# Attention heads interleaved with projections: which engine prepares weights, norms and pair parts, and in which slot each step stands

## The chip, the cores and the metric

The kernel runs on one core of a Trainium2 chip. The metric is the device time of one execution in microseconds (us). Five engines work side by side, each through its own instructions in a fixed order: TensorE (PE, with its weight loads PEld), VectorE (DVE), ScalarE (ACT), GpSimd (POOL) and SyncE (SP), which here only issues transfers between HBM and the on-chip memory, and within the latter. They wait for each other through semaphores.

## The reference

Two layers on 512 frames of 1024 channels in float32. Layer 0 mixes tokens by pooling, layer 1 by attention with 16 heads of 64 channels; both are followed by a gated MLP of width 2816. The change lies in the attention of layer 1, of which this is what must be computed:

```python
qkv = h @ w_qkv                                   # h: RMS-normed input, (512, 1024)
q, k, v = jnp.split(qkv, 3, axis=-1)
q = head_rmsnorm(q.reshape(B, S, N_HEADS, HEAD_DIM), q_norm)
k = head_rmsnorm(k.reshape(B, S, N_HEADS, HEAD_DIM), k_norm)
...
s = jnp.einsum('bqhd,bkhd->bhqk', qc, kb).astype(jnp.float32) * scale + bias[None]
s = jnp.where(valid[None, None, None, :], s, -1e30)
p = jax.nn.softmax(s, axis=-1).astype(vb.dtype)
return jnp.einsum('bhqk,bkhd->bqhd', p, vb)
...
return o @ w_o
```

A frame attends to its own chunk of 64 frames and the eight chunks before it; `bias` is a clipped relative-position table.

## The kernel before

Every float32 product is made of three fp32r products: an operand is split into a high part (`_h`, a copy rounded to fp32r) and a low part (`_l`, the rest), and `mm3` issues high times high, high times low and low times high. So each weight tile of 128x1024 that a transfer brings (`hw_r`, one per `ask(k)`) needs two further instructions, `parts(k)`: one makes `hw_h`, one subtracts and makes `hw_l`. Tiles k = 0 to 11 are those of the projections of q and k, four each for the head groups c = 1, 2, 3 (group 0 is done before); tiles 12 to 19 are those of the output product `wo`. Before, `hw_h` is made by ScalarE for k below 12 and by GpSimd for 12 to 18, and `hw_l` by GpSimd up to k = 18.

The heads run in a loop over 64 slots: slot i is head i // 4 and query tile t = i % 4 of 128 frames, with (t+1)*128 keys. A slot has two halves, and `place` counts halves. One tile's steps are spread over several slots: PE makes the scores `sc` (two matmuls, L1049 and L1050), VectorE adds the bias tile `B` and finds the maximum (L1054), ScalarE takes the exponential (L1057), VectorE the reciprocal, ScalarE scales (L1061), PE transposes into `tp` (L1065) three slots after the scores, ScalarE and VectorE copy the high and low parts out (L1069, L1071). After a head's four slots PE multiplies with the values (`oo`, L1083); a ScalarE copy and a VectorE add put two heads, a pair p, into one tile `o2` (L1090, L1094), and `split_pair` makes its high part on ScalarE (L1298) and its low part on VectorE (L1302), both in tiles named `two`. `biases(h)` issues the two transfers of a head's bias tile; there are two such tiles, for even and odd heads.

Between these steps `fill` lets PE issue matmuls of the other work, the fillers: the projections of groups 1, 2 and 3 (96 matmuls each, which end at the slots in `FE`), then `outputs()`, 144 matmuls of the output product over pairs 0 to 5. A projection's results are copied out (`copy`), squared and summed per head (`square`, `reduce`), then normed in three steps: `norm`, `seed` (ScalarE) and `better`, whose last act is to scale the four tiles `z` on GpSimd (L1199). Pairs 2c and 2c+1 come from group c.

`stages(p, i)` prepares pair p for its scores (i = 0 is q, 1 is k), in the slots that `CM` names within the eight slots of the pair before: PE transposes `z` into `zt` (L1014), ScalarE scales (L1019, `zf`) and rounds (L1021, `zh`); GpSimd copies half of `zh` (L1023, `z`) and makes the low parts (L1029 `zl` for q, L1027 `kl`, twice, for k); then two transfers from SP move halves between partitions (L1033). The second of them, `zh<-zh`, overwrites what the `kl` steps read, so it waits for both of them; the first scores of the pair, at slot 8p, wait for it.

Apart from these fixed steps, work goes through the lists `waiting`: `later(engine, fn, n)` puts it n places ahead, and `extra(engine)` lets the first entry of that engine's list be issued, in either half of a slot (a second one when the list is long). The whole loop stands in a manual schedule, so that the order of each engine's instructions is what the program writes.

```python
fillers = [(project_heads(1), 96, -3, FE[0]), (project_heads(2), 96, FE[0], FE[1]), (project_heads(3), 96, FE[1], FE[2]), (outputs(), 144, FE[2], nb + FO)]
```

## Time and profile before

| | us |
|---|---|
| median of 3 runs (lowest, highest) | 982.43 (981.92, 983.35) |
| the profiled execution: its own time | 982.51 |
| its span, first to last instruction | 980.7 |
| the stretch of the attention heads in it | 436 to 634 |
| first and last scores (slots 0 and 63) | 452.3, 606.8 |

The profiled execution's own time is 1.8 us over its span and 0.08 us over the median. Times within the span are counted from its first instruction. In rows of the timeline the columns are start, duration, engine, line, operation, output and inputs, shape, and in brackets how long the engine had been idle and what ended that. In rows by stretch, each engine has its busy time and the number of its instructions, and PEclk is the granted clock of TensorE as a share of full speed. Rows of groups have a count, the busy time in all, the mean in ns, and the idle time ahead of them.

### The profile page before, as it was taken

Reading aid. Unit: us, or ns where it says so; the run is one execution under the profiler, and the core shown is the slowest. Engines: PE = TensorE matmul, PEld = TensorE weight load, DVE = VectorE, ACT = ScalarE, POOL = GpSimd, SP = SyncE. Lnnn points to the kernel's source line nnn. Section 1 sums busy time; section 2 is a strip of 40 time slices with the busy share of each in tenths; the row PEclk is TensorE's granted clock in tenths of the full one; section 3 lists DMA queues with packets and bytes.
Section 4 is the critical chain, followed back from the end, with each engine's and each line's share of the span. In section 5 each row is a group of like instructions: output and inputs, shape, how many; then the busy total and the mean of one; then the engine's idle time right before and its main releaser. Section 6 shows DMA issues by size and latency. Waiting matters only on the chain.

```text
span 980.7 us, 13735 instructions
## 1 busy us (share of the span) xinstructions
PE 964.4 (98%) x4982; PEld 817.4 (83%) x4982; DVE 793.9 (81%) x1437; ACT 580.1 (59%) x1005; POOL 137.4 (14%) x116
## 2 busy tenths in 40 slices
PE   9999999999999999999999899999999999999998
PEld 8788988888888888888877787888988888888886
DVE  8999999999899754442665677899989999989953
ACT  7665564654565453355988798646555565556531
POOL 2300000000000022235747553100000000000000
PEclk9999999999999999999999999999999999999999
DMA  9222332332333233233334333323332332332323
GB/s 339 82 86 79 105 113 77 115 118 92 103 110 100 73 98 130 87 108 107 100 86 124 84 75 117 100 70 115 93 113 75 100 132 88 122 95 83 114 83 105
DMA packets 37427, 102.82 MB, mean 105 GB/s; under 512 B 4432, under 2 KB 7904, under 8 KB 37360
## 3 DMA queue, kind: packets, MB, share of 16 engines
q1 hardware_dynamic: 37296, 101.90, 32.7%
q8 instruction: 39, 0.64, 0.3%
q14 instruction: 28, 0.23, 0.1%
q0 software_dynamic: 32, 0.04, 0.0%
q10 hardware_dynamic: 32, 0.00, 0.0%
HBM read 95.60 MB, written 2.14 MB: 100 GB/s over the span
## 4 chain that ended last, share of the span: by engine, by line
PE 89%; DVE 6%; ACT 3%; issue 1%; DMA 1%; POOL 0%; DVEq 0%; SPq 0%; ACTq 0%; POOLq 0%
PE st_m L610 11%; PE out L124 8%; PE out L125 8%; PE out L123 8%; PE st_m L612 6%; PE st_t L610 6%; PE gv L124 3%; PE gv L125 3%; PE gv L123 3%; PE st_t L612 3%; PE st_b L610 3%; PE qk L125 3%; PE qk L123 3%; PE qk L124 3%; PE oo L1083 2%; PE v L124 1%
## 5 line engine op out<-in xcount | busy, mean ns | idle before, releaser
L124 PE MATMUL out<-one,ow_h 128*128 128x512 f32 x224 | 88.0, 393 | 0.0
L123 PE MATMUL out<-one,ow_h 128*128 128x512 f32 x224 | 87.8, 392 | 0.0
L125 PE MATMUL out<-one,ow_l 128*128 128x512 f32 x224 | 87.8, 392 | 0.0
L409 ACT ACTIVATE ow_h<-wo_r 128x640 fp32r<-128x640 f32 (+1 forms) x64 | 50.4, 788 | 56.3 <-PE out L124 46.9
L833 DVE TENSOR_TENSOR X<-out,X 128x512 f32<-128x512 f32 (+1 forms) x65 | 44.1, 679 | 48.9 <-PE out L125 48.8
L1054 DVE CUSTOM_DVE_ANT_0 sb<-sc,B 128x128 f32<-128x128 f32 (+1 forms) x64 | 31.2, 487 | 59.8 <-PE sc L1050 57.1
L610 PE MATMUL st_m<-two,g_h 128*128 128x512 f32 x240 | 75.0, 394 | 0.0
L610 PE MATMUL st_m<-h,g_h 128*128 128x512 f32 x240 | 74.0, 389 | 0.0
L410 DVE TENSOR_TENSOR ow_l<-wo_r,ow_h 128x640 fp32r<-128x640 f32 (+1 forms) x64 | 56.5, 883 | 2.6 <-ACT ow_h L409 2.6
L424 DVE SCALAR_TENSOR_TENSOR c<-a,col,c 128x511 f32<-128x511 f32 (+1 forms) x76 | 56.2, 742 | 0.0
L148 POOL TENSOR_TENSOR n_acc<-n_acc,n_sq 128x512 f32<-128x512 f32 x7 | 9.6, 1368 | 328.1 <-ACT n_sq L146 328.1
L610 PEld LDWEIGHTS st_m<-h,g_h 128*128 128x128 f32 x240 | 45.1, 188 | 10.3
L612 PEld LDWEIGHTS st_m<-two,g_l 128*128 128x128 f32 x240 | 45.0, 188 | 9.5
L610 PEld LDWEIGHTS st_m<-two,g_h 128*128 128x128 f32 x240 | 44.1, 188 | 10.0 <-ACT w L619 0.9
L619 ACT ACTIVATE w<-st_m 128x512 f32<-128x512 f32 x30 | 17.9, 598 | 57.0 <-PE st_m L612 57.0
L103 POOL TENSOR_TENSOR hw_l<-hw_r,hw_h 128x1024 fp32r<-128x1024 f32 x19 | 45.6, 2402 | 27.7 <-ACT hw_h L102 15.3
L612 PE MATMUL st_m<-h,g_l 128*128 128x256 f32 x240 | 48.3, 283 | 0.0
L125 PEld LDWEIGHTS out<-one,ow_l 128*128 128x128 f32 x224 | 42.3, 189 | 6.3
L612 PE MATMUL st_m<-two,g_l 128*128 128x256 f32 x240 | 47.6, 280 | 0.0
L124 PEld LDWEIGHTS out<-one,ow_h 128*128 128x128 f32 x224 | 42.3, 189 | 6.2 <-DVE one L435 0.3
L123 PEld LDWEIGHTS out<-one,ow_h 128*128 128x128 f32 x224 | 42.3, 189 | 6.1
L421 ACT ACTIVATE c<-a,col 128x512 f32<-128x512 f32 x38 | 30.7, 813 | 25.2 <-DVE a L768 23.6
(397 smaller groups left out, 3028.4 us busy)
## 6 DMA issues: line engine op xcount, KB each, us to landing
gv_r<-gv SPq DMA_DIRECT2D x86, 512.0 KB, 3.9
wo_r<-wout SPq DMA_DIRECT2D x32, 384.0 KB, 3.1
wo_r<-wout SPq DMA_DIRECT2D x32, 320.0 KB, 2.9
hw_r<-wqk SPq DMA_DIRECT2D x12, 512.0 KB, 3.8
wv_r<-wv SPq DMA_DIRECT2D x8, 512.0 KB, 3.3
hw_r<-wo SPq DMA_DIRECT2D x8, 512.0 KB, 4.8
xt<-xt SPq DMA_DIRECT2D x4, 512.0 KB, 5.2
X<-xT SPq DMA_DIRECT2D x8, 256.0 KB, 7.4
```

The lines of the kernel that those rows point to most:

```text
L103: return (eng or nc.vector).tensor_sub(lo, raw, hi.bitcast(F32))
L123: yield nc.tensor.matmul(o, sh, mh, start=first, stop=False, **how)
L124: yield nc.tensor.matmul(o, sh, ml, start=False, stop=False, **how)
L125: yield nc.tensor.matmul(o, sl, mh, start=False, stop=last, **how)
L409: nc.scalar.activation(hi[:, :n], raw[:, :n], AF.Copy)
L410: return hi, lo, lambda: nc.vector.tensor_sub(lo[:, :n], raw[:, :n], hi[:, :n].bitcast(F32))
L421: nc.scalar.activation(c, a, AF.Identity, scale=cw[2], bias=cw[3])
L424: nc.vector.scalar_tensor_tensor(c[:, j:], a[:, :S - j], cw[2 - j], c[:, j:], op0=OP.mult, op1=OP.add)
L610: nc.tensor.matmul(o, hi[:, c], B[i, name], start=first and i == 0, stop=False, **how)
L612: nc.tensor.matmul(o[:, 0], lo[:, c], B[i, name][:, 0], start=False, stop=i == 3, **how)
L833: nc.vector.tensor_add(X[d][:, fs], o[:, fs], X[d][:, fs])
L1054: nc.vector.tensor_tensor_reduce(out=s_, in0=sc[:, :n], in1=BT[h % 2][:, :n][:, ::-1], scale=1.0, scalar=3e38, op0=OP.add, op1=OP.min, acc ...
```

## The change

- Projections' weight tiles (k = 0 to 11, tiles 0 to 3 of them ahead of it): `hw_l` moves from GpSimd to VectorE. Output tiles 12 to 18: `hw_h` moves from GpSimd to ScalarE, `hw_l` stays on GpSimd. Past the start, both steps now go through the lists, the low part after the high part, and no longer stand at the matmul that asked for them.
- A list "G" for GpSimd. The norm's steps `norm` and `better` move from VectorE to it (7 instructions on 128x32, one more than before), and so does the pairs' low part (128x512); `norm` follows the last of the four sums, whichever that is. The GpSimd steps of `stages` are issued through it one place after ScalarE's, the transfers as many places after that so that their place stays.
- `FE` is half a slot lower: the projections end sooner by so much, and the outputs begin sooner.
- `CM`: pairs 1, 3, 5, 7 are staged one slot sooner (slots 0 and 1 of eight), pairs 2, 4, 6 one slot later (slots 2 and 3).
- Bias tiles are asked for four slots ahead of their head's first scores, where it was two.
- `outputs()` begins with three output tiles `wo0`, `wo1`, `wo2` over pairs 0 to 2, one tile after the other, then takes pair 3 for all three; before, it was two tiles in turn. The parts of weight tile 14 are asked for seven matmuls later than they would be by the rule for the others.

```diff
@@ -45,9 +45,9 @@
 LAG, LAGM = 3, 2
-FE = (3.5, 19.5, 35.5)
+FE = (3, 19, 35)
 FO = LAG + 6
-CM = (1, 2)
+CM = ((0, 1), (2, 3))
...
@@ -1107,7 +1107,8 @@
         biases(0)
-        w, raws = {}, {}
+        w, raws, ready = {}, {}, set()
+        place = 0
...
@@ -1120,7 +1121,22 @@
             w[k] = [wp.tile([P, 1024], F32R, name=f"hw{k}_{c}", tag=f"w{c}", bufs=2) for c in "hl"]
-            split(raws[k], *w[k], None if k == 19 else nc.gpsimd, nc.gpsimd if 12 <= k < 19 else None)
+            hi, lo = w[k]
+            ready.add(k)
+
+            def make_hi():
+                nc.scalar.activation(hi, raws[k], AF.Copy)
+
+            def make_lo():
+                (nc.gpsimd if 12 <= k < 19 else nc.vector).tensor_sub(lo, raws[k], hi.bitcast(F32))
+                ready.add(k)
+
+            if place == 0 or k == 19:
+                make_hi()
+                make_lo()
+            else:
+                ready.discard(k)
+                later("A", lambda: (make_hi(), later("G" if k >= 12 else "D", make_lo)))
...
@@ -1129,8 +1145,7 @@
         nb = len(tiles_)
-        place = 0
-        waiting = {"A": [], "D": [], "S": []}
+        waiting = {"A": [], "D": [], "G": [], "S": []}
...
@@ -1140,7 +1155,7 @@
             q = waiting[engine]
-            while q and q[0][0] <= place and (n == 0 or all_ or n < 2 and (place < 16 or len(q) > (1 if engine == "D" else 3))):
+            while q and q[0][0] <= place and (n == 0 or all_ or n < 2 and (place < 16 or len(q) > (1 if engine in "DG" else 3))):
...
@@ -1152,7 +1167,7 @@
             ov = {}
-            sums = {}
+            sums, summed = {}, []
...
@@ -1176,25 +1191,27 @@
                 nc.vector.tensor_reduce(three("s")[:, t, :], sq.rearrange("p (h d) -> p h d", d=HD), axis=mybir.AxisListType.X, op=OP.add)
-                if t == TT - 1:
-                    later("D", norm)
+                summed.append(t)
+                if len(summed) == TT:
+                    later("G", norm)
...
             def norm():
-                nc.vector.tensor_mul(three("a"), three("s"), r2[:, :, None].to_broadcast([P, TT, 8]))
-                nc.vector.tensor_scalar(sums["a"], sums["a"], EPS, None, op0=OP.add)
+                nc.gpsimd.tensor_mul(three("a"), three("s"), r2[:, :, None].to_broadcast([P, TT, 8]))
+                nc.gpsimd.tensor_scalar(sums["a"], sums["a"], EPS, None, op0=OP.add)
...
                 nc.scalar.activation(sums["y"], sums["t"], AF.Exp, scale=-0.5)
-                later("D", better)
+                later("G", better)
...
                 a, y, t_ = (sums[v] for v in "ayt")
-                nc.vector.scalar_tensor_tensor(t_, y, -0.5, y, op0=OP.mult, op1=OP.mult)
-                nc.vector.tensor_mul(t_, t_, a)
-                nc.vector.scalar_tensor_tensor(y, t_, 1.5, y, op0=OP.add, op1=OP.mult)
-                nc.vector.tensor_mul(three("y"), three("y"), rcol[:, :, None].to_broadcast([P, TT, 8]))
+                nc.gpsimd.tensor_mul(t_, y, y)
+                nc.gpsimd.tensor_mul(t_, t_, a)
+                nc.gpsimd.tensor_scalar(t_, t_, -0.5, 1.5, op0=OP.mult, op1=OP.add)
+                nc.gpsimd.tensor_mul(y, t_, y)
+                nc.gpsimd.tensor_mul(three("y"), three("y"), rcol[:, :, None].to_broadcast([P, TT, 8]))
...
@@ -1211,6 +1228,7 @@
                         n += 1
+                        assert k in ready
...
@@ -1222,45 +1240,31 @@
-            o = {}
+            o, left = {}, {d: len(ps_) for d in range(KD)}
+            last = ps_[-1]
+            order = [(d, p) for d in range(late) for p in ps_[:-1]] + [(d, last) for d in range(late)]
+            order += [(d, p) for d in range(late, KD) for p in ps_]
             count = 0
-
-            def product(d, p):
-                nonlocal count
-                assert p in kept
+            for d, p in order:
+                assert p in kept and k + d // nd in ready
...
                 s = slice((d % nd * len(ps_) + p - ps_[0]) * P, (d % nd * len(ps_) + p - ps_[0] + 1) * P)
-                for mm in mm3(o[d], hi[:, s], lo[:, s], XS[p], XS[KD + p], p == ps_[0], p == ps_[-1]):
+                for mm in mm3(o[d], hi[:, s], lo[:, s], XS[p], XS[KD + p], p == ps_[0], p == last):
+                    if count % 24 == 0:
+                        chunk(k + count // 24)
+                    if count % 24 == (15 if late and count // 24 == 1 else 8):
+                        parts(k + count // 24 + 1)
                     count += 1
-                    if count % 24 == 1:
-                        chunk(k + count // 24)
-                    if count % 24 == 8:
-                        parts(k + count // 24 + 1)
                     yield mm
-
-            def add(d):
-                later("D", lambda: nc.vector.tensor_add(X[d], o[d], X[d]))
-
-            for d in range(0, KD, late):
-                for p in ps_[:-1] if late > 1 and d == 0 else ps_:
-                    for e in range(d, d + late) if late > 1 and d == 0 else (d,):
-                        yield from product(e, p)
-                if late > 1 and d == 0:
-                    for e in range(late):
-                        yield from product(e, ps_[-1])
-                        add(e)
-                else:
-                    add(d)
-                    for e in range(d + 1, d + late):
-                        for p in ps_:
-                            yield from product(e, p)
-                        add(e)
+                left[d] -= 1
+                if not left[d]:
+                    later("D", lambda d=d: nc.vector.tensor_add(X[d], o[d], X[d]))
...
         def outputs():
-            yield from output_heads(range(4), 12, 2, 2)
-            yield from output_heads((4, 5), 16, 4, 1)
+            yield from output_heads(range(4), 12, 2, 3)
+            yield from output_heads((4, 5), 16, 4, 0)
...
@@ -1296,10 +1300,10 @@
                 nc.scalar.activation(XS[p], O2[p], AF.Copy)
-                later("D", lo)
+                later("G", lo)
...
             def lo():
-                nc.vector.tensor_sub(XS[KD + p], O2[p], XS[p].bitcast(F32))
+                nc.gpsimd.tensor_sub(XS[KD + p], O2[p], XS[p].bitcast(F32))
...
@@ -1325,8 +1329,11 @@
                 next(g)
+                later("G", low)
+
+            def low():
                 next(g)
-                later("S", lambda: run(g), 5 if i else 4)
+                later("S", lambda: run(g), 4 if i else 3)
...
@@ -1336,19 +1343,22 @@
                 step(i, "scores")
-                if i % 4 == 2 and i // 4 + 1 < H:
+                if i % 4 == 0 and i // 4 + 1 < H:
...
                 extra("S")
+                extra("G")
...
                 fill(i + 0.45)
-                if i % 8 in CM and i // 8 + 1 < NPAIR:
-                    stages(i // 8 + 1, CM.index(i % 8))
+                steps_at = CM[i // 8 % 2]
+                if i % 8 in steps_at and i // 8 + 1 < NPAIR:
+                    stages(i // 8 + 1, steps_at.index(i % 8))
...
                 extra("S")
+                extra("G")
...
@@ -1361,11 +1371,12 @@
                 split_pairs()
-            while waiting["A"] or waiting["D"] or cur < len(fillers):
+            while waiting["A"] or waiting["D"] or waiting["G"] or cur < len(fillers):
...
                 extra("D", True)
+                extra("G", True)
...
```

On GpSimd, from the staging of pair 3 on (`z_0`, `zl` are q's, `z_1`, `kl` are k's) to the scaling of the four tiles `z` of group 2. Before:

```order
L1023 CAST z_0_4785<-zh_0_4784 64x512
L1029 TENSOR_TENSOR zl_0_4786<-zf_0_4828,zh_0_4784 128x512
L103 TENSOR_TENSOR hw_l<-hw_r,hw_h 128x1024
L1023 CAST z_1_4826<-zh_1_4825 64x512
L1027 TENSOR_TENSOR kl_3631<-zf_1_4855,zh_1_4825 64x512
L1027 TENSOR_TENSOR kl_3632<-zf_1_4855,zh_1_4825 64x512
L1199 TENSOR_TENSOR z_0_4771<-z_0_4771,qk_y 128x512
```

Now:

```order
L1023 CAST z_0_4756<-zh_0_4755 64x512
L1029 TENSOR_TENSOR zl_0_4757<-zf_0_4800,zh_0_4755 128x512
L1023 CAST z_1_4798<-zh_1_4797 64x512
L1027 TENSOR_TENSOR kl_3631<-zf_1_4834,zh_1_4797 64x512
L1027 TENSOR_TENSOR kl_3632<-zf_1_4834,zh_1_4797 64x512
L1199 TENSOR_TENSOR qk_a<-qk_s,r_3641 128x32
L1200 TENSOR_SCALAR qk_a<-qk_a 128x32
L1210 TENSOR_TENSOR qk_t<-qk_y 128x32
L1211 TENSOR_TENSOR qk_t<-qk_t,qk_a 128x32
L1212 TENSOR_SCALAR qk_t<-qk_t 128x32
L1213 TENSOR_TENSOR qk_y<-qk_t,qk_y 128x32
L1214 TENSOR_TENSOR qk_y<-qk_y,n_y 128x32
```

The weight part between q's and k's steps is gone from GpSimd, and seven small norm steps stand ahead of the scaling.

On ScalarE, around the high part of pair 4 (`two2`), in slots 45 to 47 (`sb11_0` is head 11's tile 0, `pt0h` a high part of the transposes). Before:

```order
L1090 ACTIVATE ob9_5661<-oo9_5652 64x512
L1061 ACTIVATE sb10_3_5617<-sb10_3_5617,mx10_3_5618 128x512
L1069 ACTIVATE pt0h_3625<-tp10_2_5677 128x3x128
L1057 ACTIVATE sb11_1_5668,mx11_1_5669<-sb11_1_5668,mx11_1_5669 128x256
L1298 ACTIVATE two2_98<-o2_4_5528 128x512
L1061 ACTIVATE sb11_0_5640<-sb11_0_5640,mx11_0_5641 128x128
L1069 ACTIVATE pt0h_3625<-tp10_3_5700 128x4x128
```

Now:

```order
L1090 ACTIVATE ob9_5661<-oo9_5652 64x512
L1061 ACTIVATE sb10_3_5604<-sb10_3_5604,mx10_3_5605 128x512
L1069 ACTIVATE pt0h_3625<-tp10_2_5677 128x3x128
L1057 ACTIVATE sb11_1_5670,mx11_1_5671<-sb11_1_5670,mx11_1_5671 128x256
L1302 ACTIVATE two2_98<-o2_4_5536 128x512
L1061 ACTIVATE sb11_0_5636<-sb11_0_5636,mx11_0_5637 128x128
L1128 ACTIVATE hw14_h_5686<-hw14_r_5381 128x1024
L1069 ACTIVATE pt0h_3625<-tp10_3_5705 128x4x128
```

A weight part of 128x1024 has come in between a scaling and the next copy; such rows stand at seven places of the loop's second part (`hw12` to `hw18`).

On PE, where the output product begins (`two0` and `two4` are pair 0's high and low part). Before:

```order
L123 MATMUL wo0_0_5378<-two0_96,hw12_h_5266 128x512
L124 MATMUL wo0_0_5378<-two4_100,hw12_h_5266 128x512
L1049 MATMUL sc9_0_5383<-z24_1_5100,z24_0_5063 128x256
L1050 MATMUL sc9_0_5383<-kl01_3630,z24_0_5063 128x256
L125 MATMUL wo0_0_5378<-two0_96,hw12_l_5267 128x512
L123 MATMUL wo1_0_5397<-two0_96,hw12_h_5266 128x512
```

Now:

```order
L123 MATMUL wo0_0_5379<-two0_96,hw12_h_5264 128x512
L124 MATMUL wo0_0_5379<-two4_100,hw12_h_5264 128x512
L1065 MATMUL tp8_0_5387<-ident_106,sb8_0_5259 128x128
L125 MATMUL wo0_0_5379<-two0_96,hw12_l_5265 128x512
L123 MATMUL wo0_0_5379<-two0_96,hw12_h_5264 128x512
L1049 MATMUL sc9_0_5394<-z24_1_5127,z24_0_5092 128x256
```

The second output tile `wo1` followed after three matmuls; now nine go into `wo0` first.

## The prediction

> **What bounds the kernel now.** I read the page first, then the stretch of the heads, then what PE waited for in it, then the timeline around each wait.
>
> ```profile
> PE 964.4 (98%) x4982; PEld 817.4 (83%) x4982; DVE 793.9 (81%) x1437; ACT 580.1 (59%) x1005; POOL 137.4 (14%) x116
> 436.00:634.00 198.00, 188.44 (x989) 156.54 (x988) 122.97 (x363) 156.70 (x376) 102.15 (x73) 0.99 0.34 99
> ```
>
> PE is busy for 98% of the span, and the change removes no matmul. So time can only come from PE's idle time in the heads, 198.00 - 188.44 = 9.56 us, and from a lower clock there. PE's waits in that stretch:
>
> ```profile
> PE sc L1049 <- DMA zh<-zh: 3.1, 2, 1.7
> PE sc L1049 <- DVE qk_t L1194: 2.3, 1, 2.3
> PE wo L124 <- DVE two L1302: 1.5, 1, 1.5
> PE zt L1014 <- POOL z L1199: 0.9, 2, 0.7
> PE wo L123 <- DVE z L1161: 0.9, 1, 0.9
> PE tp L1065 <- DVE mx L1054: 0.5, 1, 0.5
> PE sc L1049 <- DVE mx L1054: 0.2, 1, 0.2
> ```
>
> They sum to 9.4 us, from several causes. The last row below, 64 bias steps from 452.8 to 608.5, gives the length of a slot: 155.7 / 63 = 2.47 us on the mean. Three of the waits are a pair's first scores (pairs 3, 5, 7):
>
> ```profile
> 508.05 2.41 POOL L103 TENSOR_TENSOR hw_l<-hw_r,hw_h 128x1024 fp32r<-128x1024 f32 x1
> 511.21 2.71 POOL L1027 TENSOR_TENSOR kl<-zf,zh 64x512 fp32r<-64x512 f32 x2
> 513.95 0.46 SPq L1033 DMA_DIRECT2D zh<-zh  x1
> 516.31 0.36 PE L1049 MATMUL sc<-zh,zh 128*128 128x256 f32 x1 [2.28 <-DVE qk_t L1194]
> ...
> 551.76 2.66 POOL L1027 TENSOR_TENSOR kl<-zf,zh 64x512 fp32r<-64x512 f32 x2
> 556.74 0.36 PE L1049 MATMUL sc<-zh,zh 128*128 128x256 f32 x1 [1.32 <-DMA zh<-zh]
> 559.47 0.80 PE L124 MATMUL wo<-two,hw_h 128*128 128x512 f32 x1 [1.47 <-DVE two L1302]
> ...
> 593.52 0.35 PE L1049 MATMUL sc<-zh,zh 128*128 128x256 f32 x1 [1.73 <-DMA zh<-zh]
> ...
> L1054 DVE CUSTOM_DVE_ANT_0 sb<-sc,B x64: 264/487/692, 452.8 to 608.5; 128x128 f32<-128x128 f32 x16, 128x256 f32<-128x256 f32 x16, 128x384 f32<-128x384 f32 x16, 128x512 f32<-128x512 f32 x16
> ```
>
> In pair 3 the named VectorE step has nothing to do with the scores: the transfer issued at 513.95, after kl ended at 513.92, and PE went on 2.36 us later. I take it for the cause. A weight part on GpSimd (2.41) stood ahead of kl. After the two waits at 556 and 559 the clock fell:
>
> ```profile
> 558.00:560.00 2.00, 0.54 (x2) 0.50 (x2) 1.72 (x9) 1.21 (x6) 1.12 (x2) 0.77 0.60 104
> 560.00:562.00 2.00, 2.00 (x8) 1.75 (x7) 0.00 (x0) 0.15 (x2) 2.00 (x3) 0.50 0.85 235
> 562.00:563.00 1.00, 1.00 (x7) 0.95 (x6) 0.00 (x0) 0.40 (x1) 1.00 (x2) 0.75 0.24 92
> ```
>
> At the granted clock of 0.50 two busy microseconds do the work of one, so 1.0 us is lost there, 0.25 in the next row and some 0.25 in PE's 0.54 of the first: 1.5 us. What the change can give back is 9.56 + 1.5 = 11.1 us. The Trainium skill ("TensorE: Matmul & The Clock Gate", Part 1) has the clock halve after an idle window of about 3.4 us; no single wait here is longer than 2.28, so by that rule the drop would not hang on these waits, and the sum below would be 1.5 less of a gain. The trace disagrees: the drop stands right behind 1.32 + 1.47 of idle time, and I keep the 1.5.
>
> **The change part by part.** The durations that move:
>
> ```profile
> L103 POOL TENSOR_TENSOR hw_l<-hw_r,hw_h 128x1024 fp32r<-128x1024 f32 x19 | 45.6, 2402 | 27.7 <-ACT hw_h L102 15.3 <-issue 11.7
> L1027 POOL TENSOR_TENSOR kl<-zf,zh 64x512 fp32r<-64x512 f32 x14 | 18.1, 1293 | 1.0
> L103 DVE TENSOR_TENSOR hw_l<-hw_r,hw_h 128x1024 fp32r<-128x1024 f32 x1 | 1.2, 1215 | 0.0
> L1302 DVE TENSOR_TENSOR two<-o,two 128x512 fp32r<-128x512 f32 x8 | 8.7, 1092 | 0.0
> L1183 DVE TENSOR_TENSOR qk_a<-qk_s,r 128x32 f32<-128x32 f32 x3 | 3.0, 1014 | 0.1
> L1023 POOL CAST z<-zh 64x512 fp32r<-64x512 f32 x14 | 8.5, 610 | 32.8 <-ACT zh L1021 28.5 <-issue 2.7 <-POOL zl L1029 0.7
> L1188 ACT ACTIVATE qk_t<-qk_a 128x32 f32<-128x32 f32 x3 | 0.7, 230 | 1.2 <-DVE qk_a L1184 1.2
> L102 ACT ACTIVATE hw_h<-hw_r 128x1024 fp32r<-128x1024 f32 x13 | 13.7, 1053 | 11.9 <-PE qk L125 6.5 <-PE v L125 4.9 <-PE wo L124 0.6
> ```
>
> GpSimd loses 12 weight low parts (12 x 2.4 = 28.8 us) and 7 high parts, and gains 8 pair parts of about 1.29 (its nearest row has 512 elements) and 21 norm instructions on 32 elements, which no row shows. From 1.293 for 512 and 2.402 for 1024 elements a line gives 0.25 us for 32; the 1.293 itself is the upper bound. I take 0.25: seven make 1.75 us a group (bounds 1.75 and 9). It was busy for 102 of 198 us, so these are latencies and not load.
>
> *Pairs 3, 5, 7* are staged a slot sooner, and no weight part stands among their GpSimd steps any more. Their three waits are 2.28 + 1.32 + 1.73. Pair 3 gains a slot, 2.47, and 2.41 of the weight part against 2.28; pair 7 gains a slot and the 2.40 of a weight part against 1.73. I let both waits go; pair 5 stays with the next item.
>
> *Group 2's scaling* (0.93 us of waits of zt).
>
> ```profile
> 512.58 0.19 DVE L1183 TENSOR_TENSOR qk_a<-qk_s,r 128x32 f32<-128x32 f32 x1
> 517.08 4.94 POOL L1199 TENSOR_TENSOR z<-z,qk_y 128x512 f32<-128x512 f32 x4 [3.15 <-DVE qk_y L1197]
> 519.45 0.33 PE L1049 MATMUL sc<-zh,zh 128*128 128x256 f32 x1
> 520.43 0.38 PE L1014 MATMUL zt<-ident,z 128*128 128x128 f32 x2
> ```
>
> From the first norm step to the scaling took 4.50 us; on GpSimd 1.75 + ScalarE's 2 x 0.23, and some for two handovers, is about 2.6. The chain begins half a slot, 1.2 us, sooner: 511.4 + 2.6 + 4.94 = 518.9. The transposes began at 520.43 in slot 25; without the 2.28 and one slot later that is 520.6. So 1.7 us in hand; at 0.5 us an instruction it is zero, at 0.61 (the nearest copy's time, of 512 elements) some of the wait remains. I leave 0.2 (0 to 0.9).
>
> *The start of the outputs* (0.91 and 1.47 us). Nine matmuls go into `wo0` before `wo1` needs its bank, and pair 3 is needed after 27 matmuls instead of 18. Both waits go, and with the pair parts off VectorE the 0.5 and 0.2 of its maximum as well. What is late next is ScalarE:
>
> ```profile
> 542.00:558.00 16.00, 13.77 (x75) 10.91 (x73) 11.96 (x35) 15.37 (x41) 8.52 (x7) 1.00 0.19 48
> 562.70:591.00 28.30, 27.65 (x160) 22.91 (x159) 21.02 (x67) 26.49 (x69) 17.45 (x15) 1.00 0.28 70
> ```
>
> From 542 to 558 it is busy for 15.37 of 16 us although PE waits there, so PE's waits let it catch up. The parts 12 and 13 bring 2 x 1.053 = 2.1 us to it in slots 33 to 38, and pair 5's zh comes in its order: kl ended at 554.42, now less than a slot sooner, some 2 us, while the scores, without the 0.91, come 0.9 sooner; I leave 0.3 of that 1.32. In all 2.2 us are left in slots 36 to 41, bounded by 0.7 (ScalarE takes the parts into its idle time) and 4.5 (they come on top of what pair 3's and 5's waits were).
>
> *Pairs 2, 4, 6* are staged a slot later; a bound of a new wait is pair 6's row:
>
> ```profile
> 562.69 0.29 PE L1049 MATMUL sc<-zh,zh 128*128 128x256 f32 x1
> 564.53 0.34 PE L1049 MATMUL sc<-zh,zh 128*128 128x384 f32 x1
> ...
> 569.18 2.64 POOL L1027 TENSOR_TENSOR kl<-zf,zh 64x512 fp32r<-64x512 f32 x2
> 571.85 0.46 SPq L1033 DMA_DIRECT2D zh<-zh  x1
> 575.33 0.28 PE L1049 MATMUL sc<-zh,zh 128*128 128x256 f32 x1
> ```
>
> It was staged at slot 41 (562.69), its transfer issued at 571.85 and by pair 3's 2.36 landed near 574.2, 11.5 us after the slot's start. Now it begins at slot 42, and from there (564.53) to slot 48 (575.33) there are 10.8 us: 0.7 is missing, and with a weight part ahead 0.8 (0 to 1.8). Pair 4's slots are longer (2.47 on the mean against 10.8 / 6 = 1.8), six of them outlast 11.5 us, and I put nothing there.
>
> *ScalarE in slots 41 to 56*: parts 14 and 15, 2.1 us, against 28.30 - 26.49 = 1.81 us of idle time, of which PE's own 0.65 of idle goes away: 0.9 is missing, less what the wait at slot 48 covers: 0.7 (0 to 2.5). Part 14's low half follows on GpSimd behind kl and a pair's part, in the same shadow.
>
> *The first tiles on VectorE*: 1.2 us each, which its 75 idle us of 198 hide. Only tile 4 is wanted at once, at slot 3: it follows ScalarE by a list's place, and a busy GpSimd can stretch it (L1302's 1.09, L1183's 1.01 for 32 elements). I put 0.5 (0 to 1.2).
>
> *Bias tiles and the end.* The transfers go from two slots ahead to four on the same SP queue; each waits for VectorE's use of the tile by the head before last, at most one slot, with the stage's transfers behind it, still 3 slots ahead of the scores. I take 0. Parts 17 and 18 go through two engines, and pair 7's low part takes 1.29 on GpSimd instead of VectorE's: 0.3 (0 to 0.9).
>
> The rule that speaks against this is the Trainium skill's ("GPSIMD Engine Reference", Engine selection), that two-input elementwise work belongs to VectorE, about twice as fast. Here L1302 took 1.09 on the mean, so 1.29 costs 0.2 a part; by the rule it is 0.65, and the sum would be worse by 0.4 for the one part on the path, pair 7's.
>
> The sum: 0.2 + 2.2 + 0.8 + 0.7 + 0.5 + 0.3 = 4.7 us of waits stay or come, 11.1 - 4.7 = 6.4 us go. From the profiled execution's 982.51 that is 976.1, against the median 0.08 less: 976.0.
>
> **The rivals.**
>
> *ScalarE becomes the bound of the second half (slower).* Its order is full from 542 on. If it sets the pace from slot 33, then the waits there (0.91, 1.32, 1.47, 0.53, 1.73 and the clock's 1.5, 7.5 us) were its own time to catch up, nothing of them returns, and seven parts add 7 x 1.053 = 7.4; the first half's 2.28 + 0.93 + 0.2 go. 982.5 + 7.4 - 3.4 = 986.5. It decides where PE's transposes wait for scaling in every head. Against it: it was idle for 2.4 us of the two stretches.
>
> *VectorE stretched.* L1302 takes 1.09 us on the mean where GpSimd works beside it, and L1183 1.01 for 32 elements. Eleven weight parts that hold up the bias step by 0.5 us each, where PE lacks a bank for it, give 5.5 back: 981.5. Against it: GpSimd has less to do, and VectorE is idle for 75 us. The Trainium skill (the same page, Key points) states such contention for VectorE instructions with two on-chip inputs, which the two rows bear out.
>
> *The even pairs come late.* All my upper bounds at slots 26, 36 to 41 and 48: 0.9 + 4.5 + 1.8 and the other 1.0 make 8.2; 11.1 - 8.2 = 2.9, 979.6.
>
> *All is covered.* Lower bounds, 0.7 left: 972.1.
>
> **How the numbers follow.** Forecast 0.47, all covered 0.18, even pairs late 0.15, VectorE stretched 0.10, ScalarE the bound 0.10. About 0.2%, or 2 us, is what a measurement of this kernel can tell from no change. Faster takes the first two and 0.13 of the third, 0.78; same 0.12; slower 0.10. From 972.5 to 982.5 only the bound of ScalarE and the best of "all covered" stay out. The forecast's own range is 974 to 978.4.
>
> **What would show it.** In the profile after: no wait of pairs 3 and 7's first scores, none of `wo` for a pair's part; the clock at 1.00 around slots 38 to 42; PE idle for about 4.7 us in the heads, with waits of transposes for ScalarE behind slot 36 and of pair 6's scores for `zh` at slot 48. Norm instructions on GpSimd of 0.25 us. I am wrong if those take 0.6, or if PE waits for ScalarE in each head of the second half.

## The result, and the profile after

| | median (lowest, highest), us | ratio to before, 95% interval |
|---|---|---|
| before, the same chip | 982.55 (981.92, 983.35), 4 runs | |
| changed | 977.51 (977.45, 977.97), 4 runs | 0.9949 [0.9932, 0.9966] |

5.0 us less; 976.0 was forecast. Two single executions of the experiments below, one of e3 (3398.93 us) and one of e6 (2467.53 us), ran in a slow state and are left out of their medians. The profiled execution took 977.97, its span is 976.2. The busy row of its page, and the stretch of the heads:

```profile
PE 963.8 (99%) x4982; PEld 815.3 (84%) x4982; DVE 796.7 (82%) x1423; ACT 585.8 (60%) x1012; POOL 120.8 (12%) x126
436.00:630.00 194.00, 188.41 (x993) 155.01 (x992) 126.03 (x350) 162.84 (x384) 85.46 (x83) 1.00 0.35 102
```

PE's busy time hardly moved (964.4 before). Its idle time in the heads fell from 9.56 to 194.00 - 188.41 = 5.59 us, 4.0 less, and the clock is at 1.00 there. The largest of PE's waits in the heads (us in all, times, longest):

```profile
PE tp L1065 <- ACT sb L1061: 2.5, 3, 1.0
```

The list of before is gone: no first scores of pairs 3, 5 or 7 wait, and `wo` waits 0.2 instead of 1.47 for pair 3. In their place stand ScalarE's scalings and short waits for VectorE and GpSimd. All of 0.2 us and more, in PE's rows of the timeline:

```profile
503.06 0.66 PE L1065 MATMUL tp<-ident,sb 128*128 128x128 f32 x4 [0.46 <-DVE mx L1054]
522.66 0.66 PE L1065 MATMUL tp<-ident,sb 128*128 128x128 f32 x4 [0.42 <-DVE o L1094]
550.16 0.44 PE L1049 MATMUL sc<-z,z 128*128 128x384 f32 x1 [0.50 <-DVE mx L1054]
553.74 0.33 PE L1065 MATMUL tp<-ident,sb 128*128 128x128 f32 x1 [0.56 <-ACT sb L1061]
556.12 0.44 PE L1065 MATMUL tp<-ident,sb 128*128 128x128 f32 x2 [0.87 <-ACT sb L1061]
561.55 0.33 PE L1014 MATMUL zt<-ident,z 128*128 128x128 f32 x1 [0.67 <-POOL z L1216]
562.77 0.50 PE L124 MATMUL wo<-two,hw_h 128*128 128x512 f32 x1 [0.22 <-POOL two L1306]
572.54 0.36 PE L1049 MATMUL sc<-zh,zh 128*128 128x256 f32 x1 [0.43 <-DMA zh<-zh]
582.60 0.44 PE L1065 MATMUL tp<-ident,sb 128*128 128x128 f32 x2 [1.01 <-ACT sb L1061]
```

Six of the nine lie between 550 and 573, in slots 38 to 48, and ScalarE's rows of the timeline show a high part of a weight tile right ahead of two of the three scalings that PE waits for (ahead of the third, at 555.57, stands pair 3's high part; L1205 is the end of the norm's seed):

```profile
552.35 1.05 ACT L1128 ACTIVATE hw_h<-hw_r 128x1024 fp32r<-128x1024 f32 x1
553.30 0.39 ACT L1061 ACTIVATE sb<-sb,mx 128x128 f32<-128x128 f32 x1
...
553.84 0.23 ACT L1205 ACTIVATE qk_y<-qk_t 128x32 f32<-128x32 f32 x1
...
581.10 1.06 ACT L1128 ACTIVATE hw_h<-hw_r 128x1024 fp32r<-128x1024 f32 x1
582.04 0.50 ACT L1061 ACTIVATE sb<-sb,mx 128x256 f32<-128x256 f32 x1
```

GpSimd at the same place, where group 3's norm stands around tile 13's low part:

```profile
551.56 0.24 POOL L1199 TENSOR_TENSOR qk_a<-qk_s,r 128x32 f32<-128x32 f32 x1
...
553.48 2.39 POOL L1131 TENSOR_TENSOR hw_l<-hw_r,hw_h 128x1024 fp32r<-128x1024 f32 x1 [1.30 <-ACT hw_h L1128]
555.83 0.24 POOL L1210 TENSOR_TENSOR qk_t<-qk_y 128x32 f32<-128x32 f32 x1
...
557.44 4.05 POOL L1216 TENSOR_TENSOR z<-z,qk_y 128x512 f32<-128x512 f32 x4
561.45 1.27 POOL L1306 TENSOR_TENSOR two<-o,two 128x512 fp32r<-128x512 f32 x1
```

ScalarE had the seed ready at 553.84 + 0.23 = 554.07, but `better` (L1210) starts at 555.83, behind the weight part: the scaling is 1.8 us later than it could be, and PE's 0.67 us wait of `zt` is for the scaling. The pair part that `wo` waits 0.22 for follows it in the same queue.

The starts of the scores by slot give the heads' length without a sum of waits. Between slots 0 and 63 lie 154.49 us before and 148.35 after. The first scores come 1.09 later (452.30 and 453.39), for two reasons: this execution was already 0.41 later ahead of the heads, in matmuls that the change does not touch, and the first projection ends half a slot sooner, so that more of its matmuls stand ahead of slot 0. The last come 5.05 sooner (606.79 and 601.74). A row of PE ahead of the heads (the projection of the values, `v`) and its first matmul behind them (the MLP's, `gv`), before and after:

```profile
436.66 1.07 PE L123 MATMUL v<-wv_h,two 128*128 128x512 f32 x4
631.77 0.39 PE L123 MATMUL gv<-one,gv_h 128*128 128x512 f32 x1
...
437.07 1.07 PE L123 MATMUL v<-wv_h,two 128*128 128x512 f32 x4
627.16 0.39 PE L123 MATMUL gv<-one,gv_h 128*128 128x512 f32 x1
```

From the one to the other it took 195.11 us before and 190.09 after, 5.02 less, which is what the medians show. Idle time is 4.0 of it, which leaves 1.0 for the clock.

### The profile page after: what moved, and what is told of

The parts are those of the page before. It is cut to its first block, busy times and chain, and to the rows that moved or that the text cites. A ratio compares the mean times of both kernels' runs of the same rounds, so it can differ in the third digit from the quotient of the medians.

```text
span 976.2 us, 13742 instructions
## 1 busy us (share of the span) xinstructions
PE 963.8 (99%) x4982; PEld 815.3 (84%) x4982; DVE 796.7 (82%) x1423; ACT 585.8 (60%) x1012; POOL 120.8 (12%) x126
## 5 line engine op out<-in xcount | busy, mean ns | idle before, releaser
L409 ACT ACTIVATE g_h<-sa 128x1024 fp32r<-128x1024 f32 x32 | 33.9, 1058 | 12.1 <-DVE sa L655 7.3
```

Of the source, the lines that this page charges most:

```text
L409: nc.scalar.activation(hi[:, :n], raw[:, :n], AF.Copy)
```

## The experiments

Each run is the changed kernel with the edit shown. "Length" is the time from the scores of slot 0 to those of slot 63 in the run's profile, "idle" is PE's idle time from 436 to 630. The heads end at another time in each run, so this stretch takes in up to some 7 us more or less of the work behind them.

| run | edit | median, us | ratio to before, 95% interval | length | idle |
|---|---|---|---|---|---|
| changed | | 977.51 | 0.9949 [0.9932, 0.9966] | 148.35 | 5.59 |
| e1 | projections' low parts on GpSimd | 980.07 | 0.9976 [0.9965, 0.9987] | 151.34 | 8.24 |
| e14 | norm on VectorE | 978.09 | 0.9951 [0.9934, 0.9967] | 148.96 | 6.14 |
| e3 | `CM` (1, 2) for all pairs | 980.41 | 0.9976 [0.9967, 0.9986] | 150.81 | 5.90 |
| e7 | `FE` of before | 978.51 | 0.9957 [0.9942, 0.9971] | 149.78 | 7.03 |
| e4 | bias tiles two slots ahead | 977.95 | 0.9951 [0.9936, 0.9966] | 148.30 | 5.51 |
| e5 | outputs' order of before | 985.53 | 1.0029 [1.0019, 1.0038] | 156.04 | 11.27 |
| e10 | that, and pairs' low parts on VectorE | 977.37 | 0.9950 [0.9934, 0.9967] | 148.64 | 5.47 |
| e6 | pairs' low parts on VectorE | 976.95 | 0.9942 [0.9925, 0.9958] | 148.22 | 5.41 |
| e2 | high parts 12 to 18 on GpSimd | 976.75 | 0.9941 [0.9925, 0.9958] | 147.69 | 5.70 |
| e9 | e2, tile 13 on VectorE | 975.62 | 0.9927 [0.9912, 0.9942] | 146.03 | 4.46 |
| e11 | e2, tile 13's parts sooner | 974.42 | 0.9915 [0.9900, 0.9929] | 145.17 | 3.60 |
| e12 | e11, tile 8 on GpSimd, pair 3 on VectorE | 974.29 | 0.9912 [0.9897, 0.9927] | 145.45 | 3.82 |

### Which engine: weight parts and norms

```diff
-                (nc.gpsimd if 12 <= k < 19 else nc.vector).tensor_sub(lo, raws[k], hi.bitcast(F32))
+                (nc.vector if k == 19 else nc.gpsimd).tensor_sub(lo, raws[k], hi.bitcast(F32))
-                later("A", lambda: (make_hi(), later("G" if k >= 12 else "D", make_lo)))
+                later("A", lambda: (make_hi(), later("G", make_lo)))
```

> The changed kernel with one part undone: the low parts of projection tiles 4 to 11 (and of 0 to 3 ahead of the slots) are made by GpSimd again, through its list. Theory A (GpSimd's weight parts ahead of kl made the pairs' first scores late, so that taking them off is a main source of the 5.0 us): group 2's scaling and pair 3's transfer come later by up to 2.4 us, PE waits 1 to 2 us more in slots 24 to 27, time 978.5 to 979.5. Theory B (the earlier staging alone was enough, and weight parts on VectorE only stretch its queue, which in the changed kernel shows as waits of 0.46 at 502 and 0.42 at 522): these two waits go, 976.6 to 977.5.

2.6 us slower than the changed kernel. The first row of PE's waits in e1:

```profile
PE qk L124 <- POOL hw_l L1131: 3.3, 3, 1.7
```

PE waited for the weight part itself, at 468, 515 and 527, a wait that I had put into neither account. On GpSimd such a part takes 2.4 us and stands behind the norm, the scaling or the staging. The 0.46 and 0.42 us of waits for VectorE at 503 and 522 did go. The intervals only just touch, and the length is 3.0 longer. So the move to VectorE gains 2.6 net of the 0.9 that it costs there.

```diff
-                    later("G", norm)
+                    later("D", norm)
-                nc.gpsimd.tensor_mul(three("a"), three("s"), r2[:, :, None].to_broadcast([P, TT, 8]))
+                nc.vector.tensor_mul(three("a"), three("s"), r2[:, :, None].to_broadcast([P, TT, 8]))
...
-                later("G", better)
+                later("D", better)
```

> The changed kernel with the norm's small steps back on VectorE (six instructions of a group instead of seven), nothing else. Theory A (GpSimd does each in about 0.25 us and one of them in 0.3 to 1.3, VectorE in 0.2 to 1.2 and behind its own queue; neither is on the path but for group 3's scaling): within 0.7 of the changed kernel, with group 3's scaling up to 1 us sooner because part 13 no longer stands ahead of the last five steps; 976.9 to 978.2. Theory B (on VectorE they stand behind weight parts of 1.4 us, ScalarE's seed waits for them and with it the scaling of the exponentials): waits of transposes for ScalarE of 1 us and more in slots 6, 22 and 38, 979 to 981.

Within 0.6 of the changed kernel, and the intervals overlap: the norm's engine makes no difference that these runs can tell. Theory A was right on the size but not on the direction at group 3. There the scaling starts at 558.00 instead of 557.44, since one step of `better` on VectorE is stretched to 1.20 us beside GpSimd.

### Which slot: staging, projections, bias tiles

```diff
-CM = ((0, 1), (2, 3))
+CM = ((1, 2), (1, 2))
```

> The changed kernel with the staging slots of before (1 and 2 of eight, for every pair). Theory A: pairs 3, 5 and 7 a slot later meet their first scores just in time at 3 and 7 (no weight part ahead of kl) but pair 5 waits 1 to 2 us; pair 4 a slot sooner waits for group 2's scaling, 1.5 to 2.5 us at slot 25, pair 6 likewise at 41: time 980 to 982. Theory B (the slots matter little, the freed GpSimd does it): 977 to 978.5.

2.9 us slower, as theory A has it. The first rows of PE's waits in e3:

```profile
PE sc L1049 <- DMA zh<-zh: 1.9, 1, 1.9
PE zt L1014 <- POOL z L1216: 1.6, 3, 0.7
```

Two stretches of e3 by engine, with the clock in the third column from the end:

```profile
552.39:555.80 3.41, 1.72 (x7) 0.87 (x6) 3.17 (x10) 3.36 (x9) 3.09 (x5) 1.00 0.47 109
555.80:559.22 3.42, 2.80 (x9) 2.33 (x10) 0.77 (x6) 3.26 (x11) 3.01 (x7) 0.50 0.75 150
```

Pair 5, staged a slot later, makes its scores wait 1.87, until 556.42, and the clock falls at 555.80, still within that wait: 2.80 x 0.50 = 1.4 us of work lost. The even pairs, staged a slot sooner, ask for the scaling too soon, though pair 4 waits only 0.57 where theory A had 1.5 to 2.5. So both halves of the rule of `CM` count, and the clock's loss comes back with the wait. Pairs 3 and 7, a slot later too, do not wait: their last transfers are issued at 513.36 and 587.17, 2.65 and 3.76 ahead of their scores, and pair 5's scores began 2.30 behind theirs.

```diff
-FE = (3, 19, 35)
+FE = (3.5, 19.5, 35.5)
```

> The changed kernel with the projections' ends of before (half a slot later), nothing else. Theory A (half a slot sooner is what lets the norms' chain of groups 2 and 3 end before the transposes of pairs 4 and 6 ask for them): zt waits for the scaling grow by about half a slot, 1.2 us a group, 0.7 + 1.2 at pair 6 and some at pair 4: 979. Theory B (the staging of the even pairs one slot later covers it, and fewer matmuls a slot in the second half help ScalarE): within 0.5 of the changed kernel, 977.5.

1.0 slower on the medians, in the direction of theory A and under its size, and the intervals overlap. (Its length counts from first scores that stand 0.7 us sooner behind the row of `v`; from that row to `gv` it took 190.90, 0.8 more than the changed kernel.) The waits of `zt` for the scaling grow from 0.7 to 1.3, and two waits of about 1 us come at 502 and 508.

```diff
-                if i % 4 == 0 and i // 4 + 1 < H:
+                if i % 4 == 2 and i // 4 + 1 < H:
```

> The changed kernel with the bias tiles asked for two slots ahead again instead of four. Theory A (the transfers land in time either way, and two slots ahead they stand beside other transfers on SP's queue than four): no wait for B in the bias steps, 977.5 within 0.5. Theory B (two slots are too short where the stages' transfers of pairs 1, 3, 5, 7 now stand sooner in the queue): VectorE waits for B at the first slots of some heads and PE with it, 978.5 to 981.

The same as the changed kernel, with the same waits to a tenth: theory A, and the 0 of the prediction.

### The output order and the pairs' low parts

```diff
-            order = [(d, p) for d in range(late) for p in ps_[:-1]] + [(d, last) for d in range(late)]
+            order = [(d, p) for p in ps_[:-1] for d in range(late)] + [(d, last) for d in range(late)]
-                    if count % 24 == (15 if late and count // 24 == 1 else 8):
+                    if count % 24 == 8:
-            yield from output_heads(range(4), 12, 2, 3)
+            yield from output_heads(range(4), 12, 2, 2)
```

> The changed kernel with the outputs' order of before: two output tiles in turn, pair 3 after 18 matmuls. Theory A: the 0.91 of the bank and the 1.47 of pair 3's low part return in part, with pair 3's part now from GpSimd: 1 to 2.5 us of PE waits in slots 36 to 40, and where two waits of over 1 us stand within 4 us the clock drops to 0.50 again and costs 1.5 more: 979 to 981. Theory B (ScalarE paces these slots anyway, 2.0 us of waits there already): the waits only change their name, 977.2 to 978.

8.0 us slower than the changed kernel, in theory A's direction and several times its size. The first row of PE's waits in e5:

```profile
PE wo L124 <- POOL two L1306: 6.5, 1, 6.5
```

GpSimd's rows of its timeline, up to the part that PE waits for:

```profile
553.01 2.37 POOL L1131 TENSOR_TENSOR hw_l<-hw_r,hw_h 128x1024 fp32r<-128x1024 f32 x1 [1.32 <-ACT hw_h L1128]
...
556.94 4.04 POOL L1216 TENSOR_TENSOR z<-z,qk_y 128x512 f32<-128x512 f32 x4
560.93 1.26 POOL L1306 TENSOR_TENSOR two<-o,two 128x512 fp32r<-128x512 f32 x1
```

And the stretch after it by engine:

```profile
562.00:570.00 8.00, 7.75 (x35) 6.81 (x36) 3.66 (x11) 3.91 (x11) 0.19 (x1) 0.70 0.00 1
```

The old order asks for pair 3 nine matmuls sooner, and on GpSimd its low part stands behind tile 13's part, `better` and four scalings. PE stops for 6.50 us, and the clock, which is at 0.50 until 566.74 and so at 0.70 on the mean of this row, costs another 7.75 x 0.30 = 2.3.

```diff
-                later("G", lo)
+                later("D", lo)
-                nc.gpsimd.tensor_sub(XS[KD + p], O2[p], XS[p].bitcast(F32))
+                nc.vector.tensor_sub(XS[KD + p], O2[p], XS[p].bitcast(F32))
```

> The changed kernel with the pairs' low parts back on VectorE, nothing else. Theory A (with the new output order VectorE has time for them, and GpSimd's queue is what delays pair 3's): the 0.22 us of wo at 562 goes, VectorE's maximum holds PE up by 0.2 to 0.5 as before: same as the changed kernel within 0.5 (977 to 978). Theory B (VectorE is stretched by eight parts of about 1.1): 1 to 2 us of waits for VectorE in the second half, 979.

976.95, theory A: the same as the changed kernel. And both edits together, that of e5 and this one:

> The changed kernel with the output product's order of before (two tiles in turn) and the pairs' low parts back on VectorE, as before. It tells whether the 6.5 us wait for pair 3's low part in the run with the old order alone comes from the order or from the engine. Theory A (engine: the part stands on GpSimd behind the norm and four scalings): the wait shrinks to about the 1.5 us it was before the change and the clock stays above half; 979, 1.5 above the changed kernel, 6.5 below the run with the order alone. Theory B (order: pair 3 is asked for too soon in any case): the wait stays above 4 us, 983 or more.

Theory A, and lower than it: 977.37. With the low part on VectorE the old order waits 0.95 for ScalarE's high part of pair 3 and 0.23 for the low part. Order and engine make a square: 985.53 (old order, GpSimd), 977.37 (old, VectorE), 977.51 (new, GpSimd), 976.95 (new, VectorE). With the old order, GpSimd costs the pair part 8 us; the new order takes them back, and the two edits together bring nothing.

### What was left: ScalarE's parts and the norm's place

```diff
-                nc.scalar.activation(hi, raws[k], AF.Copy)
+                if 12 <= k < 19:
+                    nc.gpsimd.tensor_copy(hi, raws[k])
+                else:
+                    nc.scalar.activation(hi, raws[k], AF.Copy)
-                later("A", lambda: (make_hi(), later("G" if k >= 12 else "D", make_lo)))
+                later("G", lambda: (make_hi(), make_lo())) if k >= 12 else later("A", lambda: (make_hi(), later("D", make_lo)))
```

> The changed kernel with one part undone: the high parts of output tiles 12 to 18 are made by GpSimd again, in its list just ahead of their low parts, so ScalarE has 7 x 1.05 us less. Theory A (what is left of PE's waits behind slot 36, 0.56 + 0.87 + 1.01 us on transposes, is ScalarE's extra work): these 2.4 us go, 975.0 to 976.0, and a faster kernel than the changed one. Theory B (GpSimd would be late with them as in the kernel before): part 13's 3.4 us between the norm steps delays pair 6's scaling and PE waits there 1 us more than the 0.67 now; 977.0 to 978.5.

0.8 below the changed kernel, with intervals that overlap. The waits of 0.56, 0.87 and 1.01 us for ScalarE are gone, so they did hang on its seven high parts (in e11 below, which has these on GpSimd too, PE waits for no scaling at all); but one of 1.86 has come, and its cause stands in e2's timeline, in rows of GpSimd, ScalarE and PE:

```profile
551.48 1.04 POOL L1129 CAST hw_h<-hw_r 128x1024 fp32r<-128x1024 f32 x1
552.60 2.38 POOL L1134 TENSOR_TENSOR hw_l<-hw_r,hw_h 128x1024 fp32r<-128x1024 f32 x1
554.93 0.24 POOL L1202 TENSOR_TENSOR qk_a<-qk_s,r 128x32 f32<-128x32 f32 x1
...
555.59 0.23 ACT L1207 ACTIVATE qk_t<-qk_a 128x32 f32<-128x32 f32 x1 [2.32 <-POOL qk_a L1203]
555.99 0.49 ACT L1061 ACTIVATE sb<-sb,mx 128x256 f32<-128x256 f32 x1
...
556.53 0.44 PE L1065 MATMUL tp<-ident,sb 128*128 128x128 f32 x2 [1.86 <-ACT sb L1061]
```

ScalarE, the engine that is full, stood for 2.32 us at the norm's seed, since the norm waited on GpSimd for both parts of tile 13; the scaling that PE needed was next in ScalarE's order. Two ways to take tile 13 out of there:

```diff
-                if 12 <= k < 19:
+                if k == 13:
+                    nc.vector.tensor_copy(hi, raws[k])
+                elif 12 <= k < 19:
...
+                if k == 13:
+                    later("D", lambda: (make_hi(), later("D", make_lo)))
```

> The changed kernel, with the high parts of output tiles 12 and 14 to 18 on GpSimd (as in the run that put them all there) and both parts of tile 13 on VectorE. Theory A (what is left idle around slots 36 to 42 hangs on part 13 standing between the norm's steps on GpSimd, and on ScalarE standing behind the norm's seed for it): the 1.9 us of transposes at 554, the 0.67 of zt at 560 and the 0.22 of wo go, VectorE's idle time in 549 to 559 takes the 0.7 and 1.4 us: 974.5, 2.2 below that run and 3 below the changed kernel. Theory B (VectorE, stretched, holds up the bias step instead): PE waits for VectorE's maximum or copies about 1 to 2 us in the same stretch, 976 to 977.

1.1 below e2. The 1.86 went, `zt` waits 0.20 and not 0.67, but PE waits 2.43 once for VectorE's maximum. VectorE's rows of e9's timeline:

```profile
550.16 0.84 DVE L1129 CAST hw_h<-hw_r 128x1024 fp32r<-128x1024 f32 x1
...
551.52 1.69 DVE L1136 TENSOR_TENSOR hw_l<-hw_r,hw_h 128x1024 fp32r<-128x1024 f32 x1
553.13 0.54 DVE L1054 CUSTOM_DVE_ANT_0 sb<-sc,B 128x384 f32<-128x384 f32 x1
```

Each theory was right on one place: the norm is free, and VectorE's 2.5 us stand nearly in one piece ahead of a bias step, its idle time being spread over the stretch.

```diff
-                    if count % 24 == (15 if late and count // 24 == 1 else 8):
+                    if count % 24 == ((4, 15, 8, 8)[count // 24] if late else 8):
```

> The run with the high parts 12 to 18 on GpSimd, with one edit more: the parts of output tile 13 are asked for four matmuls sooner, so that they stand on GpSimd between q's and k's steps of pair 5, where it was idle for 3.1 us, instead of ahead of the norm. Theory A (part 13 between kl and the norm holds up the norm, with it ScalarE's seed and all that stands behind it on ScalarE, and group 3's scaling): the 1.9 us of transposes at 554 shrinks to below 0.3, the 0.67 of zt and the 0.2 of wo at 561 to 563 go; pair 5's zh may come 0.3 later; idle time in 436 to 630 falls by some 2 us against that run: 974.5. Theory B (ScalarE is simply full there and the waits move on to the next slots): the idle time stays within 0.5 of that run's, 976.5.

974.42, theory A: 2.3 below e2, 3.1 below the changed kernel, 8.3 below before. Its interval lies wholly below that of the changed kernel. GpSimd's rows of e11's timeline:

```profile
545.41 1.04 POOL L1129 CAST hw_h<-hw_r 128x1024 fp32r<-128x1024 f32 x1
546.53 2.40 POOL L1134 TENSOR_TENSOR hw_l<-hw_r,hw_h 128x1024 fp32r<-128x1024 f32 x1
...
552.39 0.24 POOL L1202 TENSOR_TENSOR qk_a<-qk_s,r 128x32 f32<-128x32 f32 x1
```

The two largest of PE's waits in it:

```profile
PE sc L1049 <- DVE mx L1059: 1.1, 1, 1.1
PE sc L1049 <- DVE mx L1054: 0.6, 1, 0.6
```

The norm starts 2.5 us sooner than in e2, and no wait of transposes for ScalarE or of `zt` is left; of the stretch 550 to 563 there remain 0.58 and 1.09 of scores and 0.24 of `wo`. Against the changed kernel the length fell by 3.2 and idle time by only 2.0; the 1.2 between them is no idle time in the records, and I leave open what it is.

```diff
-                (nc.gpsimd if 12 <= k < 19 else nc.vector).tensor_sub(lo, raws[k], hi.bitcast(F32))
+                (nc.gpsimd if 12 <= k < 19 or k == 8 else nc.vector).tensor_sub(lo, raws[k], hi.bitcast(F32))
-                later("G", lo)
+                later("D" if p == 3 else "G", lo)
```

> The run before in this list, with two edits more: the low part of projection tile 8 goes to GpSimd (idle for 12 us there), and pair 3's low part to VectorE. Theory A (each removes the wait behind it: 0.46 of transposes at slot 19, where VectorE's 1.2 us for that part stands ahead of a maximum; 0.2 of wo at 562): 0.5 below the run before in this list, 974.0. Theory B (GpSimd's 2.4 us make the projection wait for its weight part, as at 466 and 525 in the run with all low parts on GpSimd): a wait of qk of 0.4 to 1.7, 975 or more.

974.29, no different from e11. The 0.46 at 503 and the 0.2 of `wo` went as theory A has it, but 0.29 of scores at 513 and 0.43 of `zt` at 560 came, and pair 6's wait grew from 0.40 to 0.66. The two edits moved waits and gained nothing.

## Why the prediction came out as it did

The sum said 11.1 us to be had, 4.7 left, 6.4 gained. The profiles show 5.59 left, so 5.5 should have been gained; from the row of `v` to that of `gv` it is 5.02, and 5.04 in the medians. The profiled execution's own time has only 4.5, as it was 0.41 late ahead of the heads.

| term | forecast left, us | measured, us |
|---|---|---|
| pairs 3 and 7's first scores | 0 | 0 |
| clock behind slots 38 to 42 | 0 | 0 (1.00) |
| slot 3, tile 4 on VectorE | 0.5 | 0 |
| group 2's scaling | 0.2 | 0 |
| slots 36 to 41, ScalarE and pair 5 | 2.2 | 0.50 + 0.56 + 0.87 = 1.93 |
| VectorE's parts at slots 18 and 26 | 0 | 0.46 + 0.42 |
| group 3's scaling, pair 3's low part | 0 | 0.67 + 0.22 |
| slot 48, pair 6 | 0.8 | 0.43 |
| slots 41 to 56, ScalarE | 0.7 | 1.01 |
| end | 0.3 | 0.16 + 0.16 |

- *The staging* was right in size, and its mechanism in part. Pairs 3 and 7 do not wait, but the prediction credits a slot and a weight part for each of them, and by e3 the slot was not needed: staged as before, without the weight part, they do not wait either (with 0.3 us to spare at pair 3). It is pair 5 that needs the slot; e3 brings back 1.87 of its wait, with a clock drop. The transfer of pair 6 was issued at 570.25 and its scores began at 572.54, 2.29 later; the 2.36 of pair 3 was the estimate.
- *ScalarE* was right in mechanism at both places, and the match of 1.93 with 1.9 (2.2 without pair 5's 0.3, which did not come) is partly luck. Waits for scalings are 0.56 + 0.87 = 1.43 of it; the 0.50 is for VectorE's maximum and stays in e2 (0.59 there), so it does not hang on the high parts. The prediction does not work its 1.9 out: parts of 2.1 less 0.63 of idle time are 1.5. Behind slot 41 it was 1.01 against 0.7. e2 confirms the cause, since all three waits go with the seven high parts. As the bound of the second half (the slower rival) it is out: it makes PE wait three times, not in each head.
- *VectorE stretched* was a rival with 5.5 us; it is a term of 0.88 that the sum lacked. The sum put the parts into 75 us of idle time, an average, where what counts is what stands behind a part in VectorE's order. A part of 2.19 us at 519.82 (its row is shown below) stands ahead of the `o` step that PE waits for at 522.66. The wait at 503 went when e12 took tile 8's part away, and that part was not stretched: it took 1.21.
- *Group 3's scaling* is the step that the sum lacked. I worked out the chain for group 2 and not for group 3, where tile 13's low part stands between `norm` and `better` on the same engine. It costs 0.67 in the changed kernel and, with the part ahead of the norm, 1.86 in e2; in e11, with the part out of the chain, the wait of `zt` is gone.
- *The start of the outputs.* The 0.91 and the 1.47 went, as forecast, but the reason was half wrong. I credited the order; by the square of e5, e10 and e6 the order only pays for the pair part on GpSimd, and in e10 the old order leaves 0.95 + 0.23 = 1.2 of the 2.4. How far the outputs' half slot sooner covers the rest was not tried.
- *The rival of late even pairs* is added up wrongly: beside its three upper bounds the other terms are 0.7 + 0.5 + 0.3 = 1.5 and not 1.0, so that it gives 980.1 and not 979.6. It did not come: pair 6 waited 0.43, pairs 2 and 4 not at all.
- *The small norm steps* took 0.22 to 0.25 us on GpSimd where 0.25 was the estimate, but for one of them, of which two in three took over 1.1. The durations of this one (shortest, median, longest):

```profile
L1200 POOL TENSOR_SCALAR qk_a<-qk_a x3: 290/1172/1290, 470.8 to 551.9; 128x32 f32<-128x32 f32 x3
```

Of the 1.5 us between forecast and median, 0.9 is the sum's (5.6 left instead of 4.7: the two missing terms add 0.88 + 0.89, and slots 3, 26, 36 to 41 and 48 took 1.3 less), 0.5 is that the heads became 5.0 shorter and not 5.5, and 0.1 is the median of before on this chip. Of the 5.0, idle time is 4.0, which leaves 1.0 where the sum has 1.5 for the clock. PE was at half speed for 3.04 busy us before, so the 1.5 itself stands; what took 0.5 back is no idle time in the records, and these profiles don't tell.

## What to carry to other kernels

Where engines run fixed orders, a step's cost is what stands behind it in its engine's order, so look for long steps put between the links of a chain across engines (here a weight part of 2.4 us between norm, seed and scaling) and ask for them some matmuls sooner, into a gap that the timeline shows. Take a change of several parts apart in pairs where one part may pay for another: undoing two of these together changes nothing, and of the two undone alone one reads as 8 us and the other as nothing. And judge spare time on an engine by the gap at the place, not by its share of a stretch.

## What the runs showed of the hardware

Where a VectorE step with two on-chip inputs and a GpSimd step overlap, the one that starts second is lengthened. The low parts of 128x1024 on VectorE in the changed kernel (shortest, median, longest):

```profile
L1131 DVE TENSOR_TENSOR hw_l<-hw_r,hw_h x13: 1207/1226/2191, 438.4 to 620.7; 128x1024 fp32r<-128x1024 f32 x13
```

The longest of them in the timeline, and GpSimd's rows beside it:

```profile
519.82 2.19 DVE L1131 TENSOR_TENSOR hw_l<-hw_r,hw_h 128x1024 fp32r<-128x1024 f32 x1
...
519.64 1.29 POOL L1306 TENSOR_TENSOR two<-o,two 128x512 fp32r<-128x512 f32 x1
520.89 2.26 POOL L1306 TENSOR_TENSOR two<-o,two 128x512 fp32r<-128x512 f32 x1
```

The first pair part started ahead of the weight part and kept its time. The weight part took 2.19 instead of 1.23, and the second pair part, which started while the weight part still ran, 2.26 instead of 1.27: each lost about as long as the other still needed. The odd norm step agrees: its two long ones, at 470.83 and 511.77, started just behind weight parts on VectorE (470.53 and 511.68). The Trainium skill ("GPSIMD Engine Reference", Key points) states that the two engines share their on-chip interfaces for such instructions, and the rows agree.

The clock did not follow the length of PE's waits. It fell to 0.50 within one of 1.87 in e3 and one of 6.50 in e5; it stayed at 1.00 with 0.67 and 1.86 within 3 us in e2 and with 2.43 in e9. Its drops have a length in common: 3.41 us before (559.10 to 562.51) and in e3 (from 555.80), and three times that in e5 (556.50 to 566.74). The stretches of this length just ahead of the drop before and of that in e5 follow (e3's, from 552.39, stands further up), and last one of e2 that no drop followed:

```profile
555.68:559.10 3.42, 1.26 (x6) 0.83 (x6) 3.19 (x11) 3.02 (x9) 2.54 (x2) 1.00 0.24 50
553.08:556.50 3.42, 1.53 (x6) 0.93 (x6) 1.72 (x8) 3.39 (x12) 3.17 (x5) 1.00 0.30 75
552.25:555.66 3.41, 1.75 (x9) 0.92 (x7) 2.15 (x7) 1.09 (x4) 3.14 (x4) 1.00 0.29 80
555.66:559.08 3.42, 2.54 (x16) 2.31 (x17) 0.55 (x3) 3.36 (x12) 2.51 (x7) 1.00 0.58 184
```

PE was busy for 0.37, 0.45 and, in e3, 0.50 of the stretch ahead of a drop, and for 0.51 in e2. Cut all fourteen traces into such stretches, in step with each trace's own changes of the clock: in the heads every one in which PE was busy for 0.50 or less is followed by half speed in the next, and none of 0.51 or more. So the place of the waits in these stretches counts beside their length. It is a reading of these traces and no run tests it by itself; the ends of matmuls are modelled, and near the end of e14 one stretch of 0.47 was followed by no drop.

The Trainium skill ("TensorE: Matmul & The Clock Gate", Part 1) has the clock halve after an idle window of about 3.4 us. The length of the drops agrees. But the stretches ahead of them were not idle: PE was busy for 1.26 us of the one before, 1.72 of e3's and 1.53 of e5's.
